# Alternating the gate and linear units of the first expert product in a one-core mixture-of-experts trunk

## The chip, the cores and the metric

The kernel runs on one core of a Trainium2 chip. The metric is the device time of one execution in microseconds, and a version's time is the median over its runs. Everything below about time is read from three runs of the kernel before and from one further execution of it, which the hardware profiler recorded.

## The reference

One layer: a modulated norm, a projection, two mixers in parallel (a recurrence and stick-breaking attention), an output projection, and then the part that this change touches, a mixture of 32 experts of which each token uses 4:

```
xb  = xt[tok]                                  # rows of one expert, gathered
hid = xb @ w1[e] + b1[e]                       # 1024 -> 2048, the first product
glu = jnp.minimum(hid[:, :1024], 7.0)          # the gate half
lin = jnp.clip(hid[:, 1024:], -7.0, 7.0)       # the linear half
act = glu * jax.nn.sigmoid(1.702 * glu) * (lin + 1.0)
y   = (act @ w2[e] + b2[e]) * gate[:, None]    # 1024 -> 1024, the second product
out[tok] += y
```

Weights are 32-bit floats: 8 MB in w1 and 4 MB in w2 for each expert.

## The kernel before

Up to about 1080 us the kernel computes the mixers and the router; then `experts` (the loop over `units`) works through the 32 experts in one order, which `expert_units` writes down. An expert has six weight tiles of 2 MB. Four belong to the first product (`w == 1`); their number `q` splits into half `q // 2` and kind `q % 2`. They are called here **G0** and **L0** (gate and linear columns of half 0) and **G1** and **L1** (of half 1). Two, **S0** and **S1**, belong to the second product (`w == 2`). Every tile is worked on in two units, `h = 0` and `h = 1`, written a and b below: G0a, G0b.

A unit of the first product (`first`) is 16 fp32r matmuls (`hid<-X,whi`) and 16 bf16 matmuls (`hid<-xb,wlo`) into one of two `hid` accumulators in PSUM; ScalarE adds the bias into `ht`, and VectorE adds the other part of the accumulator (`ht<-ht,hid`), which frees it. When the gate and the linear unit of the same columns are done, `gated` forms the activation `act` and its parts `ah`, `ab`, `al`. A unit of the second product (`second`) is `ey<-whi,ah`, `ey<-whi,al` and `ey<-wlo,ab`, apart from S0a, which multiplies the raw fp32 weights (`ey<-wraw,act`). Experts with more than 128 rows have a rest of rows, whose products `er<-wraw,act` follow the b units of S0 and S1. Large experts (144 to 184 rows) and those of 128 rows alternate for most of the phase.

Ahead of TensorE, ScalarE rounds each unit's raw weights to `whi` (`next_hi`, three units ahead, four buffers) and VectorE forms the remainder `wlo` (`next_lo`, two units ahead, three buffers). The raw tiles have four buffers, `wraw0` to `wraw3`, taken in turn in the order of `self.tiles`. SP issues the load of a tile when the buffer of four tiles earlier is free: for a tile of the first product after its second unit's `wlo`, for S0 and S1 after the second unit's matmuls. SP issues in order.

The rows of the expert after the one in the first product are prepared in `rows`, called when a unit with `t.q == 0` is worked on, which is G0: at its a unit VectorE builds the one-hot matrices `oh`, at its b unit `gather` multiplies them (`xt<-aux,oh`), VectorE turns the result into row numbers (`sa`, `si`), and GpSimd issues the indirect load `xg<-h2d,si`. `x_transpose` then transposes `xg` on TensorE (`xt<-ident,xg`); it begins at L0b, one step per unit. TensorE takes its instructions in order, and the builder places each of them by its own model of time, so the order printed below, not the loop alone, says where each stands.

The lines of the profile are 1308 (one-hot products), 1311 to 1321 (row numbers), 1327 (indirect load), 1344 (transposes), 1380 and 1386 (weight loads), 1409 (`whi`), 1427 (`wlo`), 1437 and 1441 (first product), 1447 and 1448 (bias, addition), 1498 and 1504 (second product and rest). In the changed kernel each line behind `expert_units` is 6 higher.

Of the kernel before, what the change touches and what calls it, by code (L numbers as in the profile page):

```python
# [27 lines left out]
NE = 32  # L28
# [86 lines left out]
class Trunk:  # L115
# [1241 lines left out]
    def expert_units(self, xs):  # L1357

        order = [(0, 1, q) for q in range(4)]
        for j in range(NE):
            n = [(j + 1, 1, q) for q in range(4)] if j + 1 < NE else []
            order += [*n[:1], (j, 2, 0), *n[1:2], (j, 2, 1), *n[2:]]
        tiles = [Box(x=xs[j], w=w, q=q, i=i, raw=None) for i, (j, w, q) in enumerate(order)]
        return tiles, [Box(t=t, h=h) for t in tiles for h in range(2)]

    def w_load(self, t, pool, pieces=1):
        nc, i, x = self.nc, self.i, t.x  # L1370
# [58 lines left out]
    def first(self, u, pool, psum):  # L1429

        nc, x, t = self.nc, u.t.x, u.t
        half, g = divmod(t.q, 2)
        c, f = x.c, 8 * g + 4 * half + 2 * u.h
        ps = psum.tile([128, 2, 512], FT, name="hid", bufs=2)
        for b in range(2):
            for k in range(ND):
                nc.tensor.matmul(ps[:, b, :2 * c], u.hi[:, k, b * 128:(b + 1) * 128],  # L1437
                                 x.X2[:, k].rearrange("p a c -> p (a c)"), start=k == 0, stop=False)
        for b in range(2):
            for k in range(ND):  # L1440
                nc.tensor.matmul(ps[:, b, :c], u.lo[:, k, b * 128:(b + 1) * 128], x.xb[:, k, :],  # L1441
                                 start=False, stop=k == ND - 1)
        if u.h == 0:
            x.t[g] = pool.tile([128, 4, c], FT, name="ht", bufs=3, tag="ht")
        dst = x.t[g][:, 2 * u.h:2 * u.h + 2]
        for b in range(2):
            nc.scalar.activation(dst[:, b], ps[:, b, c:2 * c], AF.Identity, bias=x.bias[:, f + b:f + b + 1])  # L1447
        nc.vector.tensor_tensor(dst, dst, ps[:, :, :c], op=OP.add)  # L1448
# [29 lines left out]
    def second(self, u, pool, psum):  # L1478


        nc, x, t = self.nc, u.t.x, u.t
        first, last = t.q == u.h == 0, t.q == u.h == 1
        n1 = self.rest(x.c)
        nj = 128 // n1 if n1 else 0
        wd = D // nj if n1 else 0
        if first:
            x.ps = [psum.tile([128, 512], FT, name="ey", bufs=2) for _ in range(2)]
            if n1:
                x.pr = psum.tile([128, 512], FT, name="er", bufs=1)
        i = 2 * t.q + u.h  # L1490
        if self.native(u):
            products = [(x.act[i], t.raw, j) for j in range(2)]
        else:
            ah, al, ab = x.parts[i]
            products = [(a, u.hi, j) for j in range(2) for a in (ah, al)] + [(ab, u.lo, j) for j in range(2)]
        for m, (a, w, j) in enumerate(products):
            for n in range(2):
                nc.tensor.matmul(x.ps[n], a[:, j, :128], w[:, j, n * 512:(n + 1) * 512],  # L1498
                                 start=first and m == 0, stop=last and m == len(products) - 1)
        if n1 and u.h == 1:  # L1500
            for k in range(4):
                a = x.act[2 * t.q + k // 2]
                for g in range(nj):
                    nc.tensor.matmul(x.pr[g * n1:(g + 1) * n1, :wd], a[:, k % 2, 128:], t.raw[:, k, g * wd:(g + 1) * wd],  # L1504
                                     start=t.q == k == 0, stop=t.q == 1 and k == 3)
        if not last:
            return
        y = pool.tile([128, D], FT, name="ey", bufs=1)
        for n in range(2):
            ns = slice(n * 512, (n + 1) * 512)  # L1510
            nc.vector.scalar_tensor_tensor(y[:, ns], x.ps[n], x.gate[:, 0:1], self.g2b[:, ns], op0=OP.mult, op1=OP.mult)  # L1511
        rows = self.out.rearrange("b s d -> (b s) d")
        nc.gpsimd.indirect_dma_start(out=rows, out_offset=bass.IndirectOffsetOnAxis(ap=x.idx[:, 0:1], axis=0),  # L1513
                                     in_=y, in_offset=None, compute_op=OP.add)
        if n1:
            yr = pool.tile([128, wd], FT, name="yr", bufs=1, tag="yr")
            nc.vector.scalar_tensor_tensor(yr, x.pr[:, :wd], x.gate[:, 1:2], self.g2r[n1], op0=OP.mult, op1=OP.mult)
            rests = self.out.rearrange("b s (j d) -> (b s j) d", j=nj)
            nc.gpsimd.indirect_dma_start(out=rests, out_offset=bass.IndirectOffsetOnAxis(ap=x.idx[:, 2:3], axis=0),
                                         in_=yr, in_offset=None, compute_op=OP.add)  # L1520
# [34 lines left out]
    def experts(self, pool, psum):  # L1555

        xs, units = self.xs, self.units
        self.ep2 = pool
        routes = self.routes(pool, psum)
        next(routes)  # L1560
        self.load()
        later, xt = [], None
        for n, u in enumerate(units):
            next(routes, None)
            self.next_hi(n + WHI - 1)
            self.next_lo(n + WLO - 1)
            later = [g for g in later if next(g, self) is not self]
            x, t = u.t.x, u.t
            if t.w == 1:
                self.first(u, pool, psum)  # L1570
                if t.q % 2:
                    g = self.gated(u, pool)
                    next(g)
                    later.append(g)
                if (t.q, u.h) == ((1, 0) if x.j else (2, 1)) and x.j + 1 < NE:
                    xt = self.x_transpose(xs[x.j + 1], (self.ep0, pool)[(x.j + 1) % 2],
                                          lambda: psum.tile([128, 512], FT, name="xt", bufs=1))
                elif t.q and xt:
                    next(xt, None)
                if t.q == 0 and 1 <= x.j < NE - 1:  # L1580
                    self.rows(xs[x.j + 1], pool, psum, u.h)
            else:
                self.second(u, pool, psum)
                if u.h == 1:
                    self.free.add(t.i)
                    self.load()
# [263 lines left out]
```

## Time and profile before

| | |
|---|---|
| median of three runs | 2486.65 us (2483.01 to 2488.38) |
| the profiled execution | 2474.98 us |
| its span in the profile | 2473.2 us |
| TensorE matmul busy | 2331.7 us, 94% of the span |
| TensorE weight load busy | 1765.6 us, 71% |
| VectorE busy | 1969.1 us, 80% |
| ScalarE busy | 1576.0 us, 64% |
| GpSimd busy | 219.5 us, 9% |
| DMA | 579.57 MB, 234 GB/s on average |

Busy time is the time in which an engine's instructions run. The profile names for an idle stretch the instruction that ended it. TensorE's granted clock is given as a share of the full 2.4 GHz. A transfer is counted from its issue to its landing.

### The profile page before, as it was taken

Reading aid. Unit: us, or ns where it says so; the run is one execution under the profiler, and the core shown is the slowest. Engines: PE = TensorE matmul, PEld = TensorE weight load, DVE = VectorE, ACT = ScalarE, POOL = GpSimd, SP = SyncE. Lnnn points to the kernel's source line nnn. Section 1 sums busy time; section 2 is a strip of 40 time slices with the busy share of each in tenths; the row PEclk is TensorE's granted clock in tenths of the full one; section 3 lists DMA queues with packets and bytes.
Section 4 is the critical chain, followed back from the end, with each engine's and each line's share of the span. In section 5 each row is a group of like instructions: output and inputs, shape, how many; then the busy total and the mean of one; then the engine's idle time right before and its main releaser. Section 6 shows DMA issues by size and latency. Waiting matters only on the chain.

```text
span 2473.2 us, 49792 instructions
## 1 busy us (share of the span) xinstructions
PE 2331.7 (94%) x19973; PEld 1765.6 (71%) x19973; DVE 1969.1 (80%) x3639; ACT 1576.0 (64%) x2467; POOL 219.5 (9%) x182
## 2 busy tenths in 40 slices
PE   6889999999999799979999999999999999999997
PEld 2456666667676665667887787888788877877875
DVE  5567568669687768678888888989888889899875
ACT  3635556557666646346676676677777777776764
POOL 0000000000000000001121111111111111121111
PEclk9989999999999799979999999999999999999999
DMA  8773343332232312567898898899899999998995
GB/s 300 268 242 114 104 118 105 112 102 83 79 106 77 107 47 93 185 213 273 302 342 279 300 362 312 313 328 363 317 314 334 343 322 323 333 365 300 320 318 158
DMA packets 321006, 579.57 MB, mean 234 GB/s; under 512 B 46526, under 2 KB 110020, under 8 KB 320740
## 3 DMA queue, kind: packets, MB, share of 16 engines
q1 hardware_dynamic: 304768, 532.21, 60.6%
q0 software_dynamic: 14304, 43.53, 7.1%
q8 instruction: 159, 2.61, 0.4%
q10 hardware_dynamic: 1700, 0.61, 0.1%
q14 instruction: 75, 0.61, 0.1%
HBM read 517.69 MB, written 58.61 MB: 233 GB/s over the span
## 4 chain that ended last, share of the span: by engine, by line
PE 70%; DMA 14%; DVE 8%; ACT 5%; issue 3%; SPq 0%; POOL 0%; POOLq 0%; ACTq 0%; DVEq 0%
PE hid L1437 14%; PE ey L1498 14%; DMA wraw<-in_exp_w_dram 8%; PE hid L1441 6%; PE rwps L660 6%; PE zps L336 4%; PE zps L338 3%; PE zps L337 3%; PE er L1504 3%; PE sbo L526 2%; DMA xg<-h2d,si 2%; ACT whi L1409 2%; PE mp L972 1%; PE sbt L523 1%; PE mp L973 1%
## 5 line engine op out<-in xcount | busy, mean ns | idle before, releaser
L1409 ACT ACTIVATE whi<-wraw 128x2048 fp32r<-128x2048 f32 (+1 forms) x361 | 675.2, 1874 | 364.3 <-PE hid L1437 167.3
L1427 DVE TENSOR_TENSOR wlo<-wraw,whi 128x2048 bf16<-128x2048 f32 (+1 forms) x361 | 804.3, 2233 | 118.2 <-PE hid L1441 73.2
L1437 PE MATMUL hid<-X,whi 128*128 128x256 f32 (+7 forms) x4096 | 622.9, 304 | 27.1 <-DVE ht L1448 25.2
L1437 PEld LDWEIGHTS hid<-X,whi 128*128 128x128 f32 x4096 | 560.6, 191 | 62.2 <-issue 44.9
L1441 PE MATMUL hid<-xb,wlo 128*128 128x128 bf16 (+7 forms) x4096 | 300.6, 227 | 0.0
L1441 PEld LDWEIGHTS <-wlo 128*128 128x128 bf16 x4096 | 253.4, 98 | 18.3 <-issue 0.3
L338 PE MATMUL zps<-hhi,zwlo 128*128 128x512 f32 x416 | 247.1, 594 | 0.0
L336 PE MATMUL zps<-hhi,zwhi 128*128 128x512 f32 x416 | 188.8, 454 | 22.1 <-DVE zlast L380 9.6
L337 PE MATMUL zps<-hlo,zwhb 128*128 128x512 bf16 x416 | 168.5, 405 | 1.4 <-DVE hlo L247 1.4
L1447 ACT ACTIVATE ht<-hid,b1r 128x128 f32<-128x128 f32 (+7 forms) x496 | 156.8, 371 | 6.1 <-PE hid L1441 5.9
L1498 PE MATMUL ey<-whi,ah 128*128 128x512 f32 x384 | 142.2, 451 | 0.0
L1448 DVE TENSOR_TENSOR ht<-ht,hid 128x256 f32<-128x256 f32 (+7 forms) x256 | 114.1, 446 | 25.6 <-ACT ht L1447 25.0
L1513 POOL DMA_INDIRECT out_dram<-ey,si x32 | 91.5, 2859 | 410.6 <-DVE ey L1511 409.4
L336 PEld LDWEIGHTS zps<-hhi,zwhi 128*128 128x128 f32 x416 | 82.7, 199 | 54.8 <-issue 22.1
L1498 PE MATMUL ey<-wraw,act 128*128 128x512 f32 x256 | 121.4, 607 | 0.0
L1498 PE MATMUL ey<-whi,al 128*128 128x512 f32 x384 | 120.6, 395 | 0.0
L1327 POOL DMA_INDIRECT xg<-h2d,si x49 | 78.8, 1609 | 406.4 <-PE ey L1498 210.2
L337 PEld LDWEIGHTS <-zwhb 128*128 128x128 bf16 x416 | 42.2, 102 | 93.5 <-issue 88.9
L1498 PE MATMUL ey<-wlo,ab 128*128 128x512 bf16 x384 | 99.6, 382 | 0.0
L514 DVE TENSOR_TENSOR_SCAN se<-se 128x128 f32<-128x128 f32 (+3 forms) x96 | 92.8, 970 | 0.7
L244 ACT ACTIVATE zwhi<-zwraw 128x1024 fp32r<-128x1024 f32 x50 | 52.8, 1055 | 60.3 <-PE zps L336 40.4
L1498 PEld LDWEIGHTS ey<-whi,ah 128*128 128x128 f32 x384 | 69.9, 189 | 28.6 <-issue 14.8
(475 smaller groups left out, 4095.3 us busy)
## 6 DMA issues: line engine op xcount, KB each, us to landing
wraw<-in_exp_w_dram SPq DMA_DIRECT2D x189, 2048.0 KB, 14.5
zwraw<-in_w_in_dram SPq DMA_DIRECT2D x50, 512.0 KB, 4.1
aw<-in_ada_w_dram SPq DMA_DIRECT2D x32, 512.0 KB, 5.7
zr<-zo SPq DMA_DIRECT2D x28, 256.0 KB, 2.3
zs<-zo SPq DMA_DIRECT2D x24, 256.0 KB, 2.1
nx<-in_x_dram SPq DMA_DIRECT2D x8, 512.0 KB, 7.1
awh<-in_ada_w_dram SPq DMA_DIRECT2D x8, 512.0 KB, 4.6
mx<-in_x_dram SPq DMA_DIRECT2D x16, 256.0 KB, 3.2
```

The costliest lines, as they stand in the source:

```text
L336: nc.tensor.matmul(ps, hi[:, k], self.hhi[:, k, s], start=k == 0, stop=False)
L337: nc.tensor.matmul(ps, hb[:, k], self.hlo[:, k, s], start=False, stop=False)
L338: nc.tensor.matmul(ps, lo[:, k], self.hhi[:, k, s], start=False, stop=k == ND - 1)
L514: nc.vector.tensor_tensor_scan(er, er, er, initial=carry, op0=OP.add, op1=OP.bypass)
L660: self.nc.tensor.matmul(out[hs], lhsT[hs], rhs[hs], start=start, stop=stop)
L1409: nc.scalar.activation(dst[:, k], src[:, k], AF.Copy)
L1427: nc.vector.tensor_tensor(dst[:, k], src[:, k], hi[:, k], op=OP.subtract)
L1437: nc.tensor.matmul(ps[:, b, :2 * c], u.hi[:, k, b * 128:(b + 1) * 128], x.X2[:, k].rearrange("p a c -> p (a c)"), start=k == 0, stop=False)
L1441: nc.tensor.matmul(ps[:, b, :c], u.lo[:, k, b * 128:(b + 1) * 128], x.xb[:, k, :], start=False, stop=k == ND - 1)
L1447: nc.scalar.activation(dst[:, b], ps[:, b, c:2 * c], AF.Identity, bias=x.bias[:, f + b:f + b + 1])
L1448: nc.vector.tensor_tensor(dst, dst, ps[:, :, :c], op=OP.add)
L1498: nc.tensor.matmul(x.ps[n], a[:, j, :128], w[:, j, n * 512:(n + 1) * 512], start=first and m == 0, stop=last and m == len(products) - 1)
```

## The change

`expert_units` lists single units instead of tiles. With `first(j, h, q)` the unit `h` of a gate tile and the unit `h` of its linear tile stand side by side. Between the first-product units of one expert stand, as before, the second-product units of the expert before it:

```
before  G0a G0b | S0a S0b | L0a L0b | S1a S1b | G1a G1b | L1a L1b
after   G0a L0a | S0a S0b | G0b L0b | S1a S1b | G1a L1a | G1b L1b
```

Tiles are numbered by their first unit, so the order of the loads becomes G0 L0 S0 S1 G1 L1, where it was G0 S0 L0 S1 G1 L1. For the very first expert the place at which the next transposes begin is written as (3, 0) instead of (2, 1), which is the same position in the list.

```diff
-        order = [(0, 1, q) for q in range(4)]
+        first = lambda j, h, q: [(j, 1, q, h), (j, 1, q + 1, h)] if j < NE else []
+        second = lambda j, q: [(j, 2, q, h) for h in range(2)]
+        order = [u for q in (0, 2) for h in range(2) for u in first(0, h, q)]
         for j in range(NE):
-            n = [(j + 1, 1, q) for q in range(4)] if j + 1 < NE else []
-            order += [*n[:1], (j, 2, 0), *n[1:2], (j, 2, 1), *n[2:]]
...
+            order += first(j + 1, 0, 0) + second(j, 0) + first(j + 1, 1, 0) + second(j, 1)
+            order += first(j + 1, 0, 2) + first(j + 1, 1, 2)
...
-                if (t.q, u.h) == ((1, 0) if x.j else (2, 1)) and x.j + 1 < NE:
+                if (t.q, u.h) == ((1, 0) if x.j else (3, 0)) and x.j + 1 < NE:
```

G0b has moved behind S0, so the one-hot products and the indirect load of the next rows, which are tied to G0b, have moved too, while the transposes are still tied to L0b. On TensorE, for an expert of 128 rows whose successor is large, from the last one-hot product to the first transposes, before:

```order
L1308 MATMUL xt<-aux,oh 32x5
L1498 MATMUL ey<-wraw_15716,act 128x512
L1437 MATMUL hid<-X_15661,whi 128x256 x16
...
L1504 MATMUL er<-wraw_15716,act 32x256 x16
L1437 MATMUL hid<-X_15661,whi 128x256 x16
...
L1437 MATMUL hid<-X_15661,whi 128x256 x16
...
L1344 MATMUL xt<-ident,xg_16007 128x128 x4
```

and in the changed kernel:

```order
L1308 MATMUL xt<-aux,oh 32x5
L1443 MATMUL hid<-X_15661,whi 128x256 x16
...
L1504 MATMUL ey<-wlo,ab 128x512
...
L1510 MATMUL er<-wraw_15773,act 32x256 x9
L1344 MATMUL xt<-ident,xg_16110 128x128 x4
L1510 MATMUL er<-wraw_15773,act 32x256 x7
```

Before, G0b, all of S0 with its rest, L0a and L0b stand between the two; now L0b, the 24 matmuls of S1 and 9 of the 16 rest matmuls do.

On VectorE, from the one-hot product's copy `sa` to the row numbers `si`, for a large expert whose successor has 128 rows, before:

```order
L1311 COPY sa<-xt 128x5
L1427 TENSOR_TENSOR wlo<-wraw_16259,whi 128x2048
L1475 TENSOR_TENSOR al<-act,ah 128x256
L1448 TENSOR_TENSOR ht<-ht,hid 128x320
L1314 SCALAR_TENSOR_TENSOR sa<-sa 128x1
L1315 TENSOR_TENSOR sa<-sa 128x1
L1296 TENSOR_SCALAR oh<-slot,keyr 128x160
L1316 TENSOR_TENSOR sa<-sa 128x1
L1318 CAST si<-sa 128x1
```

and in the changed kernel:

```order
L1433 TENSOR_TENSOR wlo<-wraw_16314,whi 128x2048 x2
L1454 TENSOR_TENSOR ht<-ht,hid 128x320
L1311 COPY sa<-xt 128x5
L1296 TENSOR_SCALAR oh<-slot,keyr 128x160
L1314 SCALAR_TENSOR_TENSOR sa<-sa 128x1
L1315 TENSOR_TENSOR sa<-sa 128x1
L1296 TENSOR_SCALAR oh<-slot,keyr 128x160
L1316 TENSOR_TENSOR sa<-sa 128x1
L1318 CAST si<-sa 128x1
```

The remainder `wlo` and the part `al` no longer stand inside this chain; the addition of G0b, which frees its accumulator, stands right ahead of it.

On SP, the loads from one S0 to the next S1, before:

```order
L1386 DMA wraw_15716<-in_exp_w_dram 128x4x1024
L1380 DMA wraw_15718<-in_exp_w_dram 128x8x512
L1386 DMA wraw_15773<-in_exp_w_dram 128x4x1024
...
L1380 DMA wraw_16091<-in_exp_w_dram 128x8x512
L1386 DMA wraw_16257<-in_exp_w_dram 128x4x1024
L1380 DMA wraw_16259<-in_exp_w_dram 128x8x512
L1386 DMA wraw_16314<-in_exp_w_dram 128x4x1024
```

and in the changed kernel:

```order
L1392 DMA wraw_15722<-in_exp_w_dram 128x4x1024
L1392 DMA wraw_15773<-in_exp_w_dram 128x4x1024
...
L1386 DMA wraw_16065<-in_exp_w_dram 128x8x512
L1386 DMA wraw_16257<-in_exp_w_dram 128x8x512
L1392 DMA wraw_16263<-in_exp_w_dram 128x4x1024
L1392 DMA wraw_16314<-in_exp_w_dram 128x4x1024
```

Shapes 128x4x1024 are S0 and S1. L0 (`wraw_15718`, `wraw_16259`) was loaded between S0 and S1; now (`wraw_16257`) it is loaded ahead of S0.

## Rows read from the trace of the kernel before

**Rows 1.** The page: the span, and TensorE's busy time with its share.

```profile
span 2473.2 us, 49792 instructions
PE 2331.7 (94%) x19973; PEld 1765.6 (71%) x19973; DVE 1969.1 (80%) x3639; ACT 1576.0 (64%) x2467; POOL 219.5 (9%) x182
```

**Rows 2.** Expert phase: busy PE, PEld, DVE, ACT, POOL; clock, DMA share, GB/s.

```profile
1144.00:2457.00 1313.00, 1279.88 (x10885) 1052.43 (x10887) 1152.24 (x1654) 931.36 (x1286) 202.63 (x151) 0.99 0.90 320
```

**Rows 3.** Waits from 1100 us on: engine, line, releaser: total us, times, longest.

```profile
PE hid L1437 <- DVE ht L1448: 25.2, 23, 2.7
...
PEld xt L1344 <- DMA xg<-h2d,si: 8.9, 8, 2.7
...
PE xt L1344 <- DMA xg<-h2d,si: 7.4, 7, 2.5
```

**Rows 4.** Timeline, a gather for 128 rows: start, us, engine, line, operation [idle before].

```profile
1443.05 0.35 PE L1308 MATMUL xt<-aux,oh 128*128 128x5 bf16 x8
...
1446.21 0.66 ACT L1447 ACTIVATE ht<-hid,b1r 128x160 f32<-128x160 f32 x2
...
1448.05 0.48 DVE L1448 TENSOR_TENSOR ht<-ht,hid 128x320 f32<-128x320 f32 x1
...
1448.83 0.15 DVE L1318 CAST si<-sa 128x1 int32<-128x1 f32 x1
...
1449.77 1.00 POOL L1327 DMA_INDIRECT xg<-h2d,si  x1 [14.01 <-PE ey L1498]
...
1457.18 0.66 PE L1344 MATMUL xt<-ident,xg 128*128 128x128 f32 x4 [0.49 <-DMA xg<-h2d,si]
```

**Rows 5.** Timeline, a gather for a large expert: product, indirect load, transposes.

```profile
1480.72 0.63 PE L1308 MATMUL xt<-aux,oh 128*128 128x5 bf16 x16
...
1490.06 1.00 POOL L1327 DMA_INDIRECT xg<-h2d,si  x1 [20.92 <-PE ey L1498]
...
1498.18 0.61 PE L1344 MATMUL xt<-ident,xg 128*128 128x128 f32 x4
```

**Rows 6.** Indirect loads from 1090 us on, issue to landing.

```profile
DMA to landing us min/median/max: 4.2/7.1/9.7
```

**Rows 7.** Chain that ended last: starts and lengths of units, second product and rest.

```profile
1467.24 2.35 PE hid L1437 x16
...
1470.71 2.39 PE hid L1437 x16
...
1492.45 2.11 PE hid L1437 x16
...
1495.47 1.96 PE hid L1437 x16
...
1498.79 5.50 PE ey L1498 x24
1504.28 1.91 PE er L1504 x32
```

**Rows 8.** Timeline and stretches of 10 us: two long waits of TensorE, and its clock.

```profile
1346.82 4.11 PE L1437 MATMUL hid<-X,whi 128*128 128x336 f32 x16 [2.67 <-DVE ht L1448]
...
1351.89 2.70 PE L1437 MATMUL hid<-X,whi 128*128 128x336 f32 x16
...
1340.00:1350.00 10.00, 7.33 (x64) 7.10 (x63) 6.88 (x10) 4.19 (x8) 1.81 (x3) 0.83 1.04 367
...
2381.91 0.66 PE L1344 MATMUL xt<-ident,xg 128*128 128x128 f32 x4 [2.54 <-DMA xg<-h2d,si]
...
2375.00:2385.00 10.00, 7.46 (x69) 6.26 (x67) 7.18 (x9) 6.77 (x10) 1.21 (x3) 1.00 1.02 380
```

**Rows 9.** Chain, then timeline: a load behind S1, its rounding, TensorE's wait, VectorE's remainder.

```profile
1506.21 11.15 DMA wraw<-in_exp_w_dram
1517.45 1.91 ACT whi L1409
...
1520.47 2.58 PE L1437 MATMUL hid<-X,whi 128*128 128x320 f32 x16 [1.49 <-DVE ht L1448]
...
1453.28 2.29 DVE L1427 TENSOR_TENSOR wlo<-wraw,whi 128x2048 bf16<-128x2048 f32 x1 [0.91 <-PE hid L1441]
```

More of the change, by code (lines that the diff above doesn't have):

```diff
@@ L1357, in expert_units @@
     def expert_units(self, xs):
-        order = [(0, 1, q) for q in range(4)]
+        first = lambda j, h, q: [(j, 1, q, h), (j, 1, q + 1, h)] if j < NE else []
+        second = lambda j, q: [(j, 2, q, h) for h in range(2)]
+        order = [u for q in (0, 2) for h in range(2) for u in first(0, h, q)]
         for j in range(NE):
-            n = [(j + 1, 1, q) for q in range(4)] if j + 1 < NE else []
-            order += [*n[:1], (j, 2, 0), *n[1:2], (j, 2, 1), *n[2:]]
-        tiles = [Box(x=xs[j], w=w, q=q, i=i, raw=None) for i, (j, w, q) in enumerate(order)]
-        return tiles, [Box(t=t, h=h) for t in tiles for h in range(2)]
+            order += first(j + 1, 0, 0) + second(j, 0) + first(j + 1, 1, 0) + second(j, 1)
+            order += first(j + 1, 0, 2) + first(j + 1, 1, 2)
+        tiles = {}
+        for j, w, q, h in order:
+            if (j, w, q) not in tiles:
+                tiles[j, w, q] = Box(x=xs[j], w=w, q=q, i=len(tiles), raw=None)
+        return list(tiles.values()), [Box(t=tiles[j, w, q], h=h) for j, w, q, h in order]
     def w_load(self, t, pool, pieces=1):
```

## The prediction

> **What bounds the kernel now.** I read the page first, for TensorE's share [rows 1], then the expert phase alone, which is where every moved instruction lies [rows 2]. There the reader is to see that TensorE's matmuls fill 1279.88 of 1313 us; 33.1 us are idle. VectorE fills 1152 us and the transfer engines are busy 90% of the time, so both run close behind, but TensorE is the engine that sets the pace. The edit takes no matmul away and adds none. What it can give is therefore at most those 33.1 us; what it can cost is any new wait of TensorE, at full length. The list of waits says what the idle time is: 25.2 us in 23 waits for an accumulator `hid`, and 8.9 us in 8 waits for the gathered rows `xg` (the weight load and the matmul record the same waits, so the 7.4 us are not added) [rows 3].
>
> The second number decides this forecast. The indirect load of the next expert's rows has almost no time in hand already: in a gather for 128 rows the one-hot product ends at 1443.40, the load is issued at 1449.77, and TensorE still waits 0.49 us for it at 1457.18, 13.8 us behind the product [rows 4]. For a large successor the same stretch is 16.8 us long, from 1481.35 to 1498.18, without a wait [rows 5].
>
> **The change, part by part.** *The gather moves, the transposes don't.* G0b, to which the one-hot product is tied, goes behind S0; the transposes stay where L0b and S1 are. The printed order of the changed kernel has 30 gathers inside the unit loop. In 10 of them the builder has set the whole product ahead of G0a; then G0a, L0a, S0, G0b and L0b follow before the transposes, more work than now, and I cost these at nothing. In the other 20 the product ends behind G0b, and what TensorE has left before the transposes can be counted:
>
> In 6 gathers (large expert, successor of 128 rows) it is L0b and about 15 of the 24 matmuls of S1. A large unit takes 3.5 us from start to start (1467.24 to 1470.71), the 24 matmuls 5.50 us [rows 7]: 3.5 + 15/24 x 5.5 = 6.9 us of cover.
>
> In 14 gathers (successor large) it is L0b, the 24 matmuls and 1 to 9 of the rest matmuls. The unit takes 3.0 us (1492.45 to 1495.47), the rest 1.91 us [rows 7]: 3.0 + 5.5 + 9/16 x 1.91 = 9.6 us, the longest of them.
>
> *What the gather needs.* Behind the product the addition into `ht` of a first-product unit comes before the row numbers in VectorE's order, then four short operations, then GpSimd. ScalarE's bias takes 0.66 us, and from the start of the addition to the issue it is 1449.77 - 1448.05 = 1.72 us [rows 4]: 2.4 us if nothing is queued. In the new order the remainder and `al` are out of this chain, which speaks for the short figure; but ScalarE has roundings of 1.9 us [rows 9] around the bias, and it is busy 931 of 1313 us [rows 2], so that a bias finds one half done on average: 0.71 x 1.91 / 2 = 0.7 us more. I take 3.1 us. As an upper end stands the chain as it is: 6.4 us to the issue for 128 rows [rows 4], 1490.06 - 1481.35 = 8.7 us for a large expert [rows 5]. From issue to landing it is 7.1 us in the median, 4.2 at best [rows 6]; the load runs beside weight loads then as now, so I take 7.1.
>
> For the 6: 3.1 + 7.1 - 6.9 = 3.3 us of wait each, 20 us. For the 14 the addition is that of L0b, 3.0 us later: 3.0 + 3.1 + 7.1 - 9.6 = 3.6 us each, 50 us. Together 70 us. Lower end: 2.4 + 4.2 us need against 6.9, and 3.0 + 2.4 + 4.2 against 9.6, no wait at all. Upper end: 6.4 + 7.1 - 6.9 = 6.6 us six times and 8.7 + 7.1 - 9.6 = 6.2 us fourteen times, 126 us. Nothing covers such a wait: TensorE takes its instructions in order, and behind the transposes stand the rest of S1 and all of the next units.
>
> *The clock.* A long wait of TensorE can cost more than its length. Behind the wait of 2.67 us at 1346.82, the granted clock over 10 us was 0.83, so part of the stretch ran at 1.2 GHz, and 16 matmuls took 4.11 us where 2.70 is usual: 1.4 us. Behind the wait of 2.54 us at 2381.91 the clock stayed at 1.00 [rows 8]. Of the five waits of 1.9 us or more in the expert phase, of which these are the first and the last, three show the loss. At three in five, 20 waits cost 20 x 0.6 x 1.4 = 17 us; the bounds are 0 and 28 us. The Trainium skill (TensorE: Matmul & The Clock Gate, What's actually happening) calls the throttled state the default, which activity releases; by that rule every long wait would pay, 28 us and a time of 2576 us. The rows bear it out in three cases of five only.
>
> *The gate work.* Activations of half 0 become ready in two steps, behind L0a and L0b, where both came behind L0b. This spreads ScalarE's and VectorE's work, but the 25.2 us of waits for `hid` do not hang on it: I read their cause in the stretch at the change of experts. A load issued at 1506.21, when S1 is done, takes 11.15 us; its rounding ends 1.9 us later, the biases stand behind it on ScalarE, and TensorE waits 1.49 us at 1520.47 [rows 9]. The new order puts L0 in the place of S0 there, ahead of the same biases. I leave these waits as they are: 0, between -25.2 (all gone) and the price in the second rival.
>
> *Loads and buffers.* L0 is issued before S0 instead of behind it; a tile of the first half stays in its buffer from its a unit to its b unit, with S0 in between, so G1's load starts two units later. Its cover is the rest of the expert's work, and I cost it at nothing. GpSimd's queue keeps its order, except that small fills now stand behind the indirect load instead of ahead of it: nothing.
>
> **The sum.** +70 for the gathers, +17 for the clock, -8.9 for the old waits for `xg`, which are these same waits: +78 us. Against the profiled execution, 2474.98 us, this is 2553 us; that execution lies 11.7 us below the median of the three runs, 2486.65 us, and on the median it is **2565 us**. The bounds of the terms give 0 + 0 - 8.9 - 25.2 = -34, no more than the idle 33.1 us can give, so 2454 us, and 126 + 28 - 9 = +145, 2632 us.
>
> **Rivals.** *The gather comes in time, and the spread work helps: faster.* With landings near the 4.2 us of the best case and an unqueued chain there is no wait, the old 8.9 us go, and if the accumulators come free sooner because the gate work is spread, up to 24 us more go. Half to all of the idle time gone is 2470 to 2454 us. It decides itself at one point: a need from product to landing below 6.9 and 9.6 us, where it is 13.8 us now [rows 4]. The landing at 4.2 us speaks for it, the median and the transfer engines' 90% against it. Chance 0.15.
>
> *The gather is late by under 1 us: no change.* The waits would then replace the old 8.9 us, about 10 to 15 us in 20 places, too short for the clock: 2487 to 2491 us. It needs both the short chain and a landing of about 4.5 us. Chance 0.07.
>
> *Weights come late as well: slower still.* At each of some 15 changes from 128 rows to a large expert, L0's load is issued when S1 ends. 11.15 us to landing, 1.91 us rounding, 2.29 us remainder [rows 9] make 15.4 us; four small units and one large one, 4 x 3.0 + 3.5 = 15.5 us [rows 7], is all the cover until L0a. Two us later each time is 30 us: 2595 us. The Trainium skill (Perfetto Trace Analysis, Identifying Performance Opportunities) reads the same gap repeated on a saturated engine as a possible lack of buffers; by that rule the four raw buffers, now held longer, would make such a gap at every expert, which no row of the kernel before shows. Chance 0.13.
>
> **The numbers.** The forecast keeps 0.65. Slower by over 0.2%, about what a measurement of this kernel can tell from no change, are the forecast and the third rival, 0.78; within it 0.07; faster 0.15. The range leaves out most of the first rival and the last part of the bounds above: 2482 to 2622 us.
>
> **What the profile will show.** If I am right, the waits for `xg` grow from 8.9 us to about 70 us, in some 20 places of 3 to 4 us each, none of them where the product stands ahead of G0a; the clock falls below 1.00 behind many of them; the waits for `hid` stay near 25 us; the landing stays near 7 us. The forecast is wrong if the waits for `xg` stay under 20 us. If they grow as said and the time doesn't, the idle time they replace was larger than I read; if the time grows without them, look at `whi` waiting for `wraw`.

## The result and the profile after

| | before | after |
|---|---|---|
| median | 2484.83 us (2481.81 to 2488.38, 4 runs) | 2619.85 us (2604.68 to 2631.78, 4 runs) |
| the profiled execution | 2474.98 us | 2623.62 us |
| its span | 2473.2 us | 2621.9 us |

The ratio is 1.0537, with a 95% interval of 1.0504 to 1.0571: 135 us slower, where 78 were forecast.

The page of the changed kernel, its span and TensorE's line, which answer to [rows 1]:

```profile
span 2621.9 us, 49501 instructions
PE 2388.8 (91%) x19805; PEld 1801.5 (69%) x19973; DVE 1981.7 (76%) x3639; ACT 1582.4 (60%) x2467; POOL 232.4 (9%) x182
```

TensorE's busy time grew too, though the edit adds no matmul. To split the rest, take the expert phase in both kernels, from the first product of a gather (`fxt<-aux,frwE`, some 8 us ahead of the first transposes) to the end of the span. The columns are the stretch and its length, busy time and instructions of PE, PEld, DVE, ACT and POOL, granted clock, DMA share, GB/s. Before:

```profile
1066.51:2473.20 1406.69, 1349.09 (x11445) 1110.13 (x11444) 1216.14 (x1822) 975.85 (x1351) 214.40 (x164) 0.99 0.88 312
```

After:

```profile
1072.99:2621.90 1548.91, 1396.19 (x11381) 1137.53 (x11444) 1228.23 (x1822) 982.46 (x1351) 227.29 (x164) 0.96 0.81 283
```

The phase is 142.2 us longer. Of these, 47.1 us are the same matmuls running slower (1396.19 - 1349.09, at a clock of 0.96 where it was 0.99; 64 matmul records are missing from the second, so it is rather a little more), and 95.1 us are idle time (152.7 against 57.6). The other 6.5 us of the span lie ahead of the phase, where nothing was edited. In all eleven kernels of this study the phase begins between 1066.51 and 1076.32, so I don't count them to the change. Figures by phase come from one execution each, and that of the kernel before is one of its quicker ones: the two spans differ by 148.7 us, the medians by 135.0.

The same stretch in all of them, worked out from such rows (idle is the stretch less the busy time), for use below:

| kernel | stretch, us | matmuls busy | idle |
|---|---|---|---|
| before | 1406.69 | 1349.09 | 57.6 |
| the change | 1548.91 | 1396.19 | 152.7 |
| the change, gather at L0a | 1512.30 | 1383.11 | 129.2 |
| before, gather at L0a (late) | 1589.68 | 1401.41 | 188.3 |
| the change, later transposes | 1505.73 | 1381.84 | 123.9 |
| the change, gather at L0a, later transposes | 1470.72 | 1373.01 | 97.7 |
| half 1 alone alternates | 1422.78 | 1349.95 | 72.8 |
| half 0 alone alternates, gather at L0a | 1527.17 | 1385.89 | 141.3 |
| the change, gather at L0a, loads by unit | 1387.89 | 1344.24 | 43.7 |
| before, loads by unit | 1386.24 | 1343.92 | 42.3 |
| the change, loads by unit | 1564.56 | 1404.75 | 159.8 |

What ended TensorE's waits in the changed kernel, and ScalarE's for the raw weights (total us, times, longest), which answer to [rows 3]:

```profile
PE xt L1344 <- DMA xg<-h2d,si: 67.7, 19, 6.2
PE hid L1443 <- DVE ht L1454: 36.0, 23, 4.0
PE hid L1443 <- DVE sa L1311: 11.6, 6, 3.7
...
PE xt L1344 <- DVE wlo L1433: 2.6, 1, 2.6
PE xt L1344 <- DVE ey L1517: 2.4, 2, 1.2
...
ACT whi L1415 <- DMA wraw<-in_exp_w_dram: 129.1, 70, 5.5
```

The waits for the gathered rows have come, 67.7 us in 19 places. But the waits for `hid` have grown as well, from 25.2 to 36.0 + 11.6 = 47.6 us, and those I had left alone. These two groups are 60.3 + 22.4 = 82.7 of the 95.1 us of new idle time. Counted in the timeline over the whole phase, waits of 1.9 us or more went from 6 to 27.

One of the six gathers for 128 rows, in order of time, which answers to [rows 4]:

```profile
1574.76 0.27 PE L1308 MATMUL xt<-aux,oh 128*128 128x5 bf16 x5
...
1575.66 0.66 ACT L1453 ACTIVATE ht<-hid,b1r 128x160 f32<-128x160 f32 x2
...
1577.24 0.48 DVE L1454 TENSOR_TENSOR ht<-ht,hid 128x320 f32<-128x320 f32 x1
...
1578.26 0.15 DVE L1318 CAST si<-sa 128x1 int32<-128x1 f32 x1
...
1578.66 2.29 DVE L1433 TENSOR_TENSOR wlo<-wraw,whi 128x2048 bf16<-128x2048 f32 x1
...
1579.19 2.63 POOL L1327 DMA_INDIRECT xg<-h2d,si  x1 [30.15 <-PE hid L1447]
...
1588.05 1.09 PE L1344 MATMUL xt<-ident,xg 128*128 128x128 f32 x4 [5.96 <-DMA xg<-h2d,si]
...
1589.36 1.05 PE L1504 MATMUL ey<-whi,ah 128*128 128x512 f32 x2
```

The chain is the one foreseen: product, bias, addition, row numbers, GpSimd, landing. The load was issued 4.16 us behind the end of the product at 1575.03 (3.1 were forecast), and the rows were there 8.86 us later (7.1 were forecast). The six waits of this kind are 5.96, 6.01, 5.95, 6.23, 5.22 and 5.97 us, 35.3 us together, where 20 were in the sum. Of the 14 for large successors, 11 end with the landing of the rows, after 1.7 to 4.9 us and 30.1 us in sum, where 3.6 us was the price of each; in the other three VectorE ended the wait (5.0 us). In sum the two misses nearly cancel. One of these three:

```profile
1632.59 1.01 POOL L1327 DMA_INDIRECT xg<-h2d,si  x1 [34.74 <-PE ey L1504]
...
1637.00 0.63 PE L1344 MATMUL xt<-ident,xg 128*128 128x128 f32 x4 [1.19 <-DVE ey L1517]
```

Here the rows were there 4.4 us behind the issue at the latest, and the gather itself cost next to nothing.

The last two of the 19 waits, 0.93 and 1.29 us, stand where none was forecast, behind a product ahead of G0a:

```profile
1994.61 0.63 PE L1308 MATMUL xt<-aux,oh 128*128 128x5 bf16 x16
...
2007.58 1.00 POOL L1327 DMA_INDIRECT xg<-h2d,si  x1 [21.65 <-PE ey L1504]
...
2016.05 0.66 PE L1344 MATMUL xt<-ident,xg 128*128 128x128 f32 x4 [0.93 <-DMA xg<-h2d,si]
```

The cover is 20.8 us here, but three remainders (`wlo`) stand inside the chain on VectorE, and the load is issued only 12.3 us behind the product.

The last row of the first gather shown, the one for 128 rows, shows the second cost: `ey` matmuls behind the wait take 1.05 us for two, where 0.63 is usual. The stretches of 10 us around it:

```profile
1570.00:1580.00 10.00, 9.95 (x82) 8.86 (x82) 7.26 (x13) 6.23 (x8) 0.81 (x1) 1.00 1.05 387
1580.00:1590.00 10.00, 3.99 (x16) 2.74 (x16) 5.12 (x8) 3.75 (x4) 1.82 (x1) 0.74 0.92 343
1590.00:1600.00 10.00, 10.00 (x78) 8.64 (x78) 7.80 (x9) 6.39 (x10) 3.37 (x1) 0.92 0.21 61
```

The granted clock of 0.74 and 0.92 says that it fell from 2.4 to 1.2 GHz for a part of the second and third stretch, while TensorE stood idle and just behind. In the third the transfer engines were busy 21% only: SP issues no weight load between 1577.35 and 1596.52. While TensorE waits, no raw buffer comes free, so the weights fall behind as well.

### The profile page after: what moved, and what is told of

It is laid out like the page before. It is cut to its first block, busy times and chain, and to the rows that moved or that the text cites. A ratio compares the mean times of both kernels' runs of the same rounds, so it can differ in the third digit from the quotient of the medians.

```text
span 2621.9 us, 49501 instructions
## 1 busy us (share of the span) xinstructions
PE 2388.8 (91%) x19805; PEld 1801.5 (69%) x19973; DVE 1981.7 (76%) x3639; ACT 1582.4 (60%) x2467; POOL 232.4 (9%) x182
## 5 line engine op out<-in xcount | busy, mean ns | idle before, releaser
L1443 PE MATMUL hid<-X,whi 128*128 128x256 f32 (+7 forms) x4096 | 634.9, 308 | 49.2 <-DVE ht L1454 36.0
L1443 PEld LDWEIGHTS hid<-X,whi 128*128 128x128 f32 x4096 | 572.1, 195 | 81.4 <-issue 59.5
L1327 POOL DMA_INDIRECT xg<-h2d,si x49 | 85.6, 1748 | 677.1 <-PE ey L1504 312.9
L337 PE MATMUL zps<-hlo,zwhb 128*128 128x512 bf16 x336 | 135.2, 402 | 1.4 <-DVE hlo L247 1.4
L1344 PE MATMUL xt<-ident,xg 128*128 128x128 f32 x290 | 50.2, 296 | 75.6 <-DMA xg<-h2d,si 67.7
L1510 PE MATMUL er<-wraw,act 128*32 128x256 f32 (+1 forms) x1088 | 105.4, 433 | 0.0
L1344 PEld LDWEIGHTS xt<-ident,xg 128*128 128x128 f32 x290 | 33.8, 150 | 88.4 <-issue 54.8
```

The lines of the kernel that those rows point to most:

```text
L337: nc.tensor.matmul(ps, hb[:, k], self.hlo[:, k, s], start=False, stop=False)
```

## The experiments

**The gather earlier, in both orders.** The first two runs move the gather alone. In the changed kernel it goes to L0a, which now stands ahead of S0; in the kernel before it goes to L0a as well, which stands behind S0 there.

```diff
-                if t.q == 0 and 1 <= x.j < NE - 1:
-                    self.rows(xs[x.j + 1], pool, psum, u.h)
+                if t.q < 2 and u.h == 0 and 1 <= x.j < NE - 1:
+                    self.rows(xs[x.j + 1], pool, psum, t.q)
```

> The changed kernel with the one-hot product and the indirect load tied to L0a instead of G0b, so that they stand ahead of S0 again; the alternating units and the load order stay. Theory (the late gather is the cause): waits for xg under 10 us, the clock back to 0.99 in the expert phase, matmul busy time there back by 40 us or more; what stays is at most the 22 us by which the waits for hid have grown: 2485 to 2515 us. Rival (weights come late because the raw tiles are held longer): the gather is no matter, 2570 us or more, with ScalarE and TensorE waiting for wraw.

> The kernel before, with its own unit and load order, and only the one-hot product and indirect load moved behind S0 (tied to L0a, which stands there in this order). Theory (late gather): in all 30 gathers 7 to 8 us of cover against a need of 13 us, so 30 waits of 4 to 6 us, 140 us, and some 45 us more through the clock: 2620 to 2680 us. Rival (the alternation and its buffers): nothing of it is here, 2485 us within 10.

The kernel before with a late gather took 2665.45 us, ratio 1.0736 (1.0704 to 1.0769): the forecast held, and the late gather by itself makes the kernel slower, without any alternation. Its waits:

```profile
PE xt L1344 <- DMA xg<-h2d,si: 141.7, 30, 6.5
```

All 30 gathers wait here, and the phase is 183 us longer than before, 6.1 us for each: 4.4 us of idle time and 1.7 us of slower matmuls. That is a net price: the waits for `hid` fell to 4.2 us, and new waits of `ey` for `wraw` add 17.5 us. In the change 20 are late, so 120 us at this price, an estimate and rather a high one, since the 20 wait 3.5 us each there and the 30 here 4.7.

The changed kernel with an early gather took 2588.05 us, ratio 1.0432 (1.0408 to 1.0455). That is a miss: it should have come back to about the kernel before, and gained 32 us only; the waits for `xg`, expected under 10 us, are still 30.1. So the alternation has a second cost, which shows when the first is taken away:

```profile
PE hid L1443 <- DVE sa L1311: 37.0, 11, 4.8
PE hid L1443 <- DVE ht L1454: 31.7, 21, 4.5
PE xt L1344 <- DMA xg<-h2d,si: 30.1, 9, 6.0
...
ACT whi L1415 <- DMA wraw<-in_exp_w_dram: 137.0, 66, 5.4
```

The waits for `hid` are now 68.7 us. One of them in the timeline of this run, at a change from 128 rows to a large expert, in order of time:

```profile
1629.01 1.93 PE L1510 MATMUL er<-wraw,act 128*32 128x256 f32 x32
...
1631.00 0.37 SPq L1386 DMA_DIRECT2D wraw<-in_exp_w_dram  x1
...
1643.12 1.91 ACT L1415 ACTIVATE whi<-wraw 128x2048 fp32r<-128x2048 f32 x1 [4.48 <-DMA wraw<-in_exp_w_dram]
1644.94 0.87 ACT L1453 ACTIVATE ht<-hid,b1r 128x128 f32<-128x128 f32 x3
...
1645.06 2.29 DVE L1433 TENSOR_TENSOR wlo<-wraw,whi 128x2048 bf16<-128x2048 f32 x1 [4.09 <-ACT whi L1415]
...
1647.61 0.41 DVE L1454 TENSOR_TENSOR ht<-ht,hid 128x256 f32<-128x256 f32 x1
...
1648.17 4.61 PE L1443 MATMUL hid<-X,whi 128*128 128x320 f32 x16 [4.47 <-DVE sa L1311]
```

S1's last product ends at 1630.94; at 1631.00 the load of the next expert's L0 is issued into the buffer that S1 has left. ScalarE comes to round it long before it has landed, stands for 4.48 us, and the biases of units that are already computed stand behind it. VectorE stands the same way in the remainder, with the additions behind it. So both accumulators stay full, and TensorE waits, not for L0 but for `hid`, in G0a, a unit that has its weights. Of the 68.7 us, 40.9 are waits of G0a and 18.0 of G1b. The 16 matmuls behind the wait take 4.61 us, where 2.58 is usual.

**The transposes later, and both.** The next two runs leave the loads as they are and give the gather time at its other end: the transposes begin at G1a, behind S1, and no longer at L0b ahead of it.

```diff
-                if (t.q, u.h) == ((1, 0) if x.j else (3, 0)) and x.j + 1 < NE:
+                if (t.q, u.h) == ((1, 1) if x.j else (3, 0)) and x.j + 1 < NE:
```

> The changed kernel with the transposes begun one unit later (at G1a), gather still behind G0b. Theory (what counts is the distance from gather to transposes): cover grows by a unit of 3.0 to 3.5 us and what is left of S1, to 12 to 14 us, about the need: waits for xg 0 to 20 us, 2490 to 2530 us. Rival (weights late): no change from the changed kernel, 2600 us or more.

> The changed kernel with the gather at L0a and the transposes begun at G1a: the widest distance, over 20 us. Theory (late gather): no wait for xg at all; what is left is the alternation alone with its waits for hid: 2475 to 2510 us, and within 10 us of the run with the gather at L0a. Rival (weights late): 2570 us or more.

Both are misses. Late transposes alone: 2570.78 us, ratio 1.0352 (1.0326 to 1.0379). With the early gather too: 2535.99 us, ratio 1.0220 (1.0191 to 1.0249). The waits of the first:

```profile
PE hid L1443 <- DVE X L1354: 69.5, 17, 6.2
PE xt L1344 <- DMA xg<-h2d,si: 13.0, 14, 3.1
```

and of the second:

```profile
PE hid L1443 <- DVE X L1354: 36.3, 15, 4.6
PE hid L1443 <- DVE ht L1454: 21.5, 21, 3.1
...
```

The waits for `xg` are as low as expected, 13.0 us in the first run and none in the second; the times are not. In the first run the wait stands one step further on: the next expert's first product waits for `X`, whose copies come out of the same ScalarE and VectorE queues. What remains in the second run, 64 us of phase, can't be the gather, whose rows no instruction waits for there.

**Which half, and whether it is the load.** Two runs alternate one half only (with `whole(j, q)` for the two units of a tile; the one that alternates half 0 has the gather at L0a as well), and two cut every weight load into its units.

```diff
+        whole = lambda j, q: [(j, 1, q, h) for h in range(2)] if j < NE else []
...
-            order += first(j + 1, 0, 0) + second(j, 0) + first(j + 1, 1, 0) + second(j, 1)
+            order += whole(j + 1, 0) + second(j, 0) + whole(j + 1, 1) + second(j, 1)
             order += first(j + 1, 0, 2) + first(j + 1, 1, 2)
```

> Only half 1 alternates (G1a L1a G1b L1b); half 0, its loads, the gather and the transposes stand as before the change. What is open is why the gather at L0a still left 109 us over the kernel before. Theory, weights late: L0's load, which waits for S1's buffer, is asked for too early by the rounding on ScalarE; this order keeps L0's load as before, so 2465 to 2500 us, and ScalarE's waits for wraw stay near the 108 us of before. Rival, the alternation itself: the gate work of half 1 spread between its units holds up the biases, so about half of the 109 us: 2520 to 2560 us.

```diff
             order += first(j + 1, 0, 0) + second(j, 0) + first(j + 1, 1, 0) + second(j, 1)
-            order += first(j + 1, 0, 2) + first(j + 1, 1, 2)
+            order += whole(j + 1, 2) + whole(j + 1, 3)
...
```

> The complement: half 0 alternates, with the gather at L0a, and half 1 stands as before (G1a G1b L1a L1b). L0 is loaded ahead of S0, into the buffer that S1 frees. Weights late: nearly all of the 109 us are here, 2560 to 2600 us, as waits for hid at the changes of expert, with ScalarE waiting for wraw over 125 us. Rival, the alternation itself: about half, 2520 to 2560 us.

Half 1 alone: 2498.91 us, ratio 1.0061 (1.0033 to 1.0089), as expected. Half 0 alone: 2606.07 us, ratio 1.0497 (1.0464 to 1.0531), 6 us above the range expected. ScalarE's waits for `wraw` in the kernel before:

```profile
ACT whi L1409 <- DMA wraw<-in_exp_w_dram: 107.8, 51, 4.0
```

They rose to 137.0 us with half 1 alone, against the expectation, and TensorE's waits for `hid` there are:

```profile
PE hid L1444 <- DVE ht L1455: 37.1, 32, 4.5
...
```

and TensorE's waits with half 0 alone:

```profile
PE hid L1444 <- DVE ht L1455: 63.7, 27, 5.7
PE xt L1344 <- DMA xg<-h2d,si: 40.2, 12, 6.4
```

The cost lies in half 0. Alone it costs 120.5 us of phase (1527.17 against 1406.69), more than both halves together, 105.6 us; alternating gate and linear units in half 1 costs 16.1 us. That speaks against the alternation as such, and for the loads of half 0. The sum of ScalarE's waits for `wraw`, 137.0 us without harm and 121.4 us with it (over 125 were expected), doesn't tell the two runs apart. Whose load it waits for does. ScalarE rounds in the order of the units, so each wait can be given to its unit by counting; the last two columns are the median time from the issue of a load to the moment at which ScalarE has nothing left ahead of its rounding:

| kernel | waits at G1a, us | at L0a, us | G1, us | L0, us |
|---|---|---|---|---|
| before | none | 51.9 in 18 | 15.7 | 13.2 |
| the change | 37.2 in 14 | 31.2 in 16 | 6.3 | 8.9 |
| the change, gather at L0a | 45.1 in 15 | 45.8 in 16 | 5.7 | 9.0 |
| half 1 alone alternates | 9.0 in 4 | 68.5 in 22 | 15.7 | 10.3 |
| half 0 alone alternates, gather at L0a | 58.5 in 23 | 39.3 in 17 | 6.6 | 10.2 |

So L0's load is not the only one. G1's goes into the buffer that G0 leaves, and where half 0 alternates G0 stays until G0b, behind S0. One such place with half 0 alone, a rounding of G1a that waits during S1 and TensorE's wait two units into half 1, at L1a:

```profile
1764.28 3.71 ACT L1416 ACTIVATE whi<-wraw 128x2048 fp32r<-128x2048 f32 x2 [4.84 <-DMA wraw<-in_exp_w_dram]
...
1780.45 4.20 PE L1444 MATMUL hid<-X,whi 128*128 128x320 f32 x16 [5.37 <-DVE ht L1455]
```

With half 0 alone 27.1 us of the waits for `hid` are in G0a and 32.9 us in L1a. No run moves one of the two loads without the other, so their shares stay open.

The cut: each unit has its own 1 MB load and its own half buffer, eight of them in the same memory.

```diff
-WRAW, WHI, WLO = 4, 4, 3
+WRAW, WHI, WLO = 8, 4, 3
...
-        raw = pool.tile([128, ND * 512], FT, name="wraw%d" % (t.i % WRAW), bufs=1)
+        raw = pool.tile([128, ND * 256], FT, name="wraw%d" % (u.i % WRAW), bufs=1)
...
-                                                               w[:, k:k + n, g, half * 512:(half + 1) * 512])
+                                                                    w[:, k:k + n, g, c:c + 256])
...
-            if u.h == 1 and u.t.w == 1:
-                self.free.add(u.t.i)
+            if u.t.w == 1:
+                self.free.add(u.i)
                 self.load()
...
-                    self.free.add(t.i)
+                    self.free.update((u.i - 1, u.i))
```

> The gather at L0a, as in the first run, and every 2 MB load cut into its two units' 1 MB, eight raw buffers of half the size: a unit's load then starts when the unit eight places ahead is done with its raw weights, and waits for no other. Weights late: the residual of 109 us goes, 2465 to 2510 us, and ScalarE's waits for wraw fall under 60 us. Rival, the alternation itself: the order of units is that of the first run, so 2560 to 2600 us.

> The kernel before with the same loads by unit, as the control: what the cut does without any alternation. If 1 MB loads with runs of 1 KB move as fast as 2 MB loads, the buffers come free sooner and the 25 us of waits for hid shrink: 2455 to 2480 us. If the shorter runs cost bandwidth, the transfer engines, busy 90 % of the phase, become the bound: over 2520 us, and then the run before says little.

The alternation with the early gather and these loads took 2466.3 us, ratio 0.9931 (0.9911 to 0.995), the kernel before with these loads 2460.33 us, ratio 0.9904 (0.9872 to 0.9937). The first run:

```profile
PE xt L1344 <- DMA xg<-h2d,si: 7.3, 4, 2.8
PE hid L1446 <- DVE sa L1311: 5.8, 7, 1.7
PE hid L1446 <- DVE ht L1457: 5.3, 12, 0.9
...
ACT whi L1418 <- DMA wraw<-in_exp_w_dram: 40.5, 30, 2.4
```

and its control:

```profile
PE hid L1440 <- DVE ht L1451: 13.4, 15, 1.9
...
```

Both expectations held. The order of units is that of the run at 2588.05 us; the loads alone take 122 us off it, and ScalarE waits neither at G1a nor at L0a any more. The alternation as such costs nothing that this can tell: the medians are 6 us apart and the two intervals overlap. And both versions beat the kernel before, the control by 22 us (2482.41 in the same runs).

**The change with the weights cured.** The last run gives the change, its late gather included, the loads by unit.

> The change as it is, its late gather too, with the loads cut by unit: the weights come in time, so what is left is the price of the gather alone. In this build all 30 gathers of the loop stand behind S0, where 20 did in the change. By the price of the prediction, 3.3 to 3.6 us of wait and 0.85 us of clock each, it is 30 x 4.3 = 129 us over the 2466 us of the same order with an early gather: 2570 to 2620 us, with the waits for xg near 100 us. By the price that the run of the kernel before with a late gather showed, 186 us for 30, it is 2630 to 2665 us. Rival, the gather is late only because the weights are (L0's load and the rounding ahead of its chain): under 2520 us, waits for xg under 30 us.

It took 2644.78 us, ratio 1.0644 (1.0609 to 1.0678). TensorE's waits:

```profile
PE xt L1344 <- DMA xg<-h2d,si: 134.4, 30, 7.2
...
PE hid L1446 <- DVE ht L1457: 0.6, 1, 0.6
```

One of its gathers in the timeline:

```profile
1691.64 0.34 PE L1308 MATMUL xt<-aux,oh 128*128 128x5 bf16 x8
...
1695.86 2.29 DVE L1436 TENSOR_TENSOR wlo<-wraw,whi 128x2048 bf16<-128x2048 f32 x1
...
1696.07 2.95 POOL L1327 DMA_INDIRECT xg<-h2d,si  x1 [26.49 <-PE hid L1450]
...
1706.20 1.09 PE L1344 MATMUL xt<-ident,xg 128*128 128x128 f32 x4 [7.17 <-DMA xg<-h2d,si]
```

The waits for `hid` are gone and the gather costs its full price: the phase is 176.7 us longer than with the same loads and the early gather, 5.9 us for each of 30 (3.9 us of idle time and 2.0 us of slower matmuls). The price that the kernel before with a late gather gave is right, the prediction's 4.3 too small, and the rival, a gather that is late only because the weights are, has fallen.

So each cause was shown alone: the late weights cost 105.6 us of phase (early gather, loads as in the change; the 30.1 us of waits for `xg` in that run are among them, and fall to 7.3 with the loads by unit), the late gather 5.9 to 6.1 us in each place, up to some 120 us for the 20 of the change. Together they cost 142.2 us, not 225. The likely reason is that the loads and the roundings catch up while TensorE stands at a gather, so that the wait for `hid` that would have come next is shorter: 47.6 us where 68.7 came with the early gather, and 4.2 where 25.2 came in the kernel before.

## Why the prediction was right, and where it was off

The sign, the main mechanism and the range held. That the range held, by 2 us, owes something to luck: two terms left their bounds or their zero, the clock (47.1 us, bounds 0 and 28) and the waits for `hid` (22.4 us more, costed at 0), and they found room only because the gathers stayed far below their upper end of 126 us. Step by step:

- *The gather.* Right in mechanism and in sum: 67.7 us in 19 places, against 70 in 20. That the sum is so near is luck, since the two prices were off in opposite directions. The term "3.3 us" of the six gathers measured 5.9. Of the 2.6 us missing in the one shown, 1.06 are the chain (4.16 to the issue against 3.1), and 1.76 the time from issue to landing (8.86 against 7.1), nearly all of which is GpSimd's own instruction, 2.63 us where it took 1.00 in [rows 4]; the cover was 0.2 us longer than reckoned. The term "3.6 us" of the fourteen measured 2.7 in 11 places: their rows were there 5.35 to 7.58 us behind the issue, in 10 of the 11 sooner than the median of 7.1 that I took for all. The landing did not stay near 7 us, its median fell to 5.4. And "none of them where the product stands ahead of G0a" failed twice, by 2.2 us in sum.
- *The clock.* The mechanism was right, the size was not: +17 us forecast, +47.1 us of slower matmuls measured. There were 21 more waits of 1.9 us or more, about as many as forecast, but each costs 47.1 / 21 = 2.2 us, if all of it is put down to them, not 0.85. One step to this is a misreading: four of the five waits of the kernel before show the loss, not three. Behind the one of 2.19 us at 2099.45 the granted clock over 10 us was 0.83, and 16 bf16 matmuls took 1.93 us where 1.07 is usual. That makes 20 x 0.8 x 1.4 = 22 us, still too little. The price of 1.4 us was read from the 16 matmuls directly behind a wait of 2.67 us [rows 8]; behind the longer waits here the slower clock reaches further (2.03 us in the 16 fp32r matmuls alone behind a wait of 4.47 us). By the rule of the Trainium skill that was weighed there (TensorE: Matmul & The Clock Gate, What's actually happening: the throttled state is the default) every long wait pays, which gave 28 us: nearer, borne out in four cases of five, and still too little, since it was priced by the same row.
- *Loads and buffers, and the 25.2 us of waits for `hid`.* Both were costed at nothing; this step is wrong. The waits for `hid` grew by 22.4 us, and by 43.5 us with the early gather. "Its cover is the rest of the expert's work" was said of G1's load, rightly seen to start later, but with TensorE in mind. ScalarE asks three units ahead of TensorE, and the time that a load has until then fell from 15.7 to 6.3 us for G1 and from 13.2 to 8.9 us for L0, against a landing of 11 us (median of the weight loads: 11.0). For L0 this is the question at G1b: between it and S1, which frees the buffer, stand only G1a and L1a. Whoever stands behind that question waits too. The prediction had this chain in [rows 9], put L0 into it, and left the waits as they were (the upper price that it refers to there is that of its third rival, not the second). The runs with loads by unit show that it is the loads, and the half-by-half runs that it is half 0.
- *The third rival, weights late as well,* happened, beside the forecast and not in its place. Its price of 30 us was too low: without the late gather it is 105.6 us. Its reasoning measured the cover to L0a on TensorE, 15.5 us against a need of 15.4, missed that the wait falls on G0a, a unit earlier, and left out G1. The page it leant on (the Trainium skill, Perfetto Trace Analysis, Identifying Performance Opportunities: a repeated gap on a saturated engine as a possible lack of buffers) points to the right place, and the trace agrees: with buffers that come free unit by unit the waits for `hid` fall from 68.7 to 11.1 us.
- *The first two rivals,* a gather in time or late by under 1 us, have fallen: the 19 waits run from 0.9 to 6.2 us, and 17 of them are over 1.6 us.

## What to carry to other kernels

Before units are reordered, write down for every buffer who frees it and who asks for it first, with the engine that works ahead included, and measure the time between: here it fell from 15.7 to 6.3 us for one tile in six and from 13.2 to 8.9 us for another, and ScalarE, which waited in order, passed its wait on to work that was ready. Fix that distance first (smaller loads, freed one by one); with that, the order hardly mattered here. And price a new wait of TensorE above its length: in the seven kernels here that lost over 60 us each added us of idle time came with 0.4 to 0.6 us of slower matmuls, and two causes of new waits cost less together than their sum.

## What was not expected of the hardware

- GpSimd's instruction for the indirect load takes about 1.0 us in some places and 1.9 to 5.0 us in others, and VectorE's remainder tells which. Over the kernel before, the change and the last run, 69 of the 70 that took over 1.2 us began while a remainder was running, and none of the 77 shorter ones did; the one exception took 1.36 us. The 69 end 0.8 to 1.3 us after that remainder or after the next one; in the gathers shown it is 0.87 us both times (1581.82 against 1580.95, 1699.02 against 1698.15). In [rows 4], 1.00 us, the next remainder began 0.32 us later. The rows land later by it: of the six gathers for 128 rows, the one with 1.01 us has them 7.35 us behind the issue, the other five, 2.47 to 2.94 us, 8.85 to 9.22 us. The Trainium skill (GPSIMD Engine Reference, Specifications) says that GpSimd's way to SBUF is shared with VectorE and contended by its instructions with two SBUF inputs. The remainder has two, and these rows agree. No run here took the remainder away, so the cause is read, not shown.
- The slower clock cost about half as much again as the idle time that went with it, wherever the waits were long: 47.1 us of matmul time for 95.1 us of idle time in the change, 34.0 for 71.6 with the early gather, 52.3 for 130.7 in the kernel before with the late one, 55.7 for 102.2 in the last run (differences to the row of before in the table). In the run that alternates half 1, with 15.2 us of added idle time, it cost 0.9 us. No run kept TensorE busy through a wait, so that the waits cause it is argued from these rows.
- Loads of 1 MB, with runs of 1 KB for the first product where they were 2 KB, keep the transfer engines busier for the same bytes: 0.96 at 316 GB/s where the kernel before shows 0.88 at 312. It did no harm here.
